# A hybrid decoder step on one core: sums of squares and two S5 table products moved from GpSimd to VectorE

## Chip, cores and metric

The kernel runs on 1 core of one Trainium2 chip. The metric is the device time of one execution in microseconds (us), taken as the median of several runs. A run is an execution of the whole program: one decoder layer for a prompt of 1024 tokens and a sample batch of 8 x 4 tokens, 1056 token columns in all.

The engines are TensorE (PE; its weight loads are PEld), VectorE (DVE), ScalarE (ACT), GpSimd (POOL) and SyncE (SP, which issues most DMAs). Each runs its own list of instructions in order and waits on semaphores for the others.

## The reference, cut to what matters here

One layer: an RMS norm, one input projection into attention, S5 and gate columns, attention and the S5 state-space branch, gates, output projection, MLP, final norm.

```python
def rmsnorm(x, g):
    xf = x.astype(jnp.float32)
    y = xf * lax.rsqrt(jnp.mean(xf * xf, axis=-1, keepdims=True) + RMS_EPS)
    return (y * g.astype(jnp.float32)).astype(x.dtype)
...
def s5_discretize(lam_re, lam_im, log_dt, b_re, b_im):
    """ZOH: A_bar = exp(dt*Lambda), B_bar = (A_bar - 1)/Lambda * B."""
...
    bb_re = f_re * b_re - f_im * b_im
    bb_im = f_re * b_im + f_im * b_re
    return ab_re, ab_im, bb_re, bb_im
...
    h = rmsnorm(x, g_mix)
    proj = h @ w_in
    q, k, v, u, gate_logits = jnp.split(
        proj, [D_ATTN, D_ATTN + D_KV, D_ATTN + 2 * D_KV, D_ATTN + 2 * D_KV + D_SSM], axis=-1)
```

The change touches the sum of the squares of x (for the norm), the product with `f_im` in `bb_re` and `bb_im`, and the product with the imaginary part of a power of `A_bar` that carries the sample states over four steps.

## The kernel before

Activations lie transposed: a tile has 128 of the 1024 channels as partitions and the 1056 tokens as columns, so x is eight tiles (k = 0 to 7). A product is made from three matmuls per k and chunk of 352 columns: high part of the weight by high part of the activation (L117), high by low (L118), low by high (L119). So each tile of x has a high part `hh` (ScalarE, L181, times the norm's weight) and a low part `hl` (VectorE, L182), and each weight block of 128x1024 a high part (ScalarE, L91) and a low part (VectorE, L92).

The part of the program that the change touches is its beginning:

- `start` (L166) loads x, makes `hh` and `hl`, squares each tile on ScalarE (L186) into one of three buffers `sq` and adds the squares up in `acc` (L188), on GpSimd.
- `first_tiles` (L500) multiplies two gate tiles with k outermost: for each k 18 matmuls of 128x352, 144 in all, into six banks of PSUM. So k waits for `hl[k]`.
- `token_norms` (L191) sums `acc` over the partitions on TensorE (L198), takes the root (L157 on ScalarE, the rest on VectorE) and spreads the result `r` over the partitions with TensorE (L207) into `rb`.
- `s5_params` (L266) is a long list of small VectorE instructions (64 or 32 columns) that discretise the state-space model; nine doublings of an angle (L374 to L381) are its end.
- `tile_in` (L506) makes one further tile of the projection: three banks of 24 matmuls each. Behind the first gate tiles come a gate tile and then the u tiles, whose banks VectorE moves out (`u_evac`, L435), times `rb`. Three banks (`mm`) go round, so the fourth u bank waits for nothing older than the first u bank, and the first bank of the third u tile for the evacuation of the fourth.
- `s5_tables` (L385) makes the table BB and the carried states FS, each from two products and a sum; one of the two products ran on GpSimd (L391, L402).
- `s5_a` (L537) and `s5_b` (L572) make per group of eight the matrices W2, V1, W1 and Kp, with a product on GpSimd beside VectorE each (L556, L568). Their memory (`s5work`) is that of the temporaries of `s5_params`, so the first `s5_a` waits for the last doubling. `s5_phases` (L404) makes tables of phases on VectorE (L420 to L425).

A scheduler sets the order of each engine's list when the program is built, from priorities and its own idea of how long things take; so an edit of an engine moves other instructions too. The numbers behind the names (mm_953, acc_174) tell tiles apart.

Of the kernel before, what the change touches and what calls it, by code (L numbers as in the profile page):

```python
# [12 lines left out]
ALU = mybir.AluOpType  # L13
# [32 lines left out]
def hybrid_kernel(tc, xt, cache_k, cache_v, h0, norms, w_in, sinks, w_attn_o, lam_re, lam_im, log_dt,  # L46
                  b_ri, b_ir, c_ri, d_cols, w_glu, w_out, w_up, w_down, w_last,
                  y_cols, y_rows, k_prompt, v_prompt, ssm_prompt, k_sample, v_sample, ssm_sample, dbg=None):
    nc = tc.nc
    uid = [0]  # L50

    def new(pool, shape, dt, tag, bufs=None):
        uid[0] += 1
        return pool.tile(list(shape), dt, tag=tag, name=f"{tag}_{uid[0]}", bufs=bufs)
# [47 lines left out]
    def prefetch(pool=wts):  # L102

        if len(loaded) < len(cols_in):
            kind, m = cols_in[len(loaded)]
            loaded.append(wblock(w_in, CB[kind] + m, pool=pool))
# [59 lines left out]
    def start(st, small_loads):  # L166

        nc.scalar.dma_start(gcol, norms)
        acc = new(st, [P, T], F32, "acc")
        xs = []  # L170
        for k in range(KT):
            x = new(st, [P, T], F32, "x", 8)
            nc.sync.dma_start(x, xt[k])
            if k in (0, PF2):
                prefetch(wts if k else st)
            if k == PF3:
                prefetch()
            if k == SLK:
                small_loads()
            g = gcol[:, 0, k:k + 1]  # L180
            nc.scalar.activation(hh[k], x, AF.Copy, scale=g)  # L181
            nc.vector.scalar_tensor_tensor(hl[k], x, g, hh[k].bitcast(F32), op0=ALU.mult, op1=ALU.subtract)  # L182
            xs.append(x)
        for k, x in enumerate(xs):
            sq = new(st, [P, T], F32, "sq", 3) if k else acc
            nc.scalar.activation(sq, x, AF.Square)  # L186
            if k:
                (nc.vector if k in AV else nc.gpsimd).tensor_tensor(acc, acc, sq, op=ALU.add)  # L188
        return acc

    def token_norms(st, acc):  # L191
# [17 lines left out]
            nc.scalar.copy(rb[:, 3 * c * P:3 * c * P + w], ps[:, :w])  # L209

    PF3 = 5
    AV, PF2, SLK = (), 1, 1


    AR0, AI0, R8 = 0, 9, 18
# [15 lines left out]
    def swap(dst, src, s0=1.0, s1=1.0):  # L231

        for d, s, sg in ((dst[0:64], src[64:128], s0), (dst[64:128], src[0:64], s1)):
            if sg == 1.0:
                nc.scalar.copy(d, s)
            else:
                nc.scalar.activation(d, s, AF.Copy, scale=sg)

    def s5_small_loads(pt):
        lr, li, ldt = (new(pt, [P, G], F32, t) for t in ("lr", "li", "dt"))  # L240
        nc.sync.dma_start(ldt, bass.AP(tensor=log_dt.tensor, offset=log_dt.offset, ap=[[0, P], [1, G]]))
        nc.sync.dma_start(lr, lam_re)
        nc.sync.dma_start(li, lam_im)
        return lr, li, ldt

    def s5_loads(pt):
        Y = new(slabA, [P, G, CH], F32, "slab")
        Ys = new(slabA, [P, G, CH], F32, "slab")
        dcol = new(pt, [P, KT, 2], F32, "dcol")
        q = S5Q  # L250
        q.dma_start(dcol, d_cols)
        q.dma_start(Y, b_ri)
        q.dma_start(Ys, b_ir)
        q.dma_start(XC, c_ri)
        q.dma_start(H0, h0)
        nc.gpsimd.memset(Up, 0.0)
        nc.gpsimd.memset(BBp, 0.0)
        nc.gpsimd.memset(Kp, 0.0)
        m16 = new(pt, [P, CH], F32, "m16")
        for i in range(4):  # L260
            nc.gpsimd.tensor_copy(m16[32 * i:32 * i + 32], ident[32 * i:32 * i + 32, 32 * i:32 * i + CH])
        nc.gpsimd.tensor_tensor(DD, m16[:, None, None, :].to_broadcast([P, KT, 2, CH]),
                                dcol[:, :, :, None].to_broadcast([P, KT, 2, CH]), op=ALU.mult)
        return Y, Ys
# [120 lines left out]
    def s5_tables(Y, Ys, fr, fi):  # L385
        nc.scalar.activation(XC[64:128], XC[64:128], AF.Copy, scale=-1.0)
        nc.scalar.activation(Ys[0:64], Ys[0:64], AF.Copy, scale=-1.0)

        sh = [P, G, CH]
        nc.vector.tensor_tensor(BB, Y, fr[:, :, None].to_broadcast(sh), op=ALU.mult)  # L390
        nc.gpsimd.tensor_tensor(Ys, Ys, fi[:, :, None].to_broadcast(sh), op=ALU.mult)  # L391
        nc.vector.tensor_tensor(BB, BB, Ys, op=ALU.add)

        H0s = new(slabA, [P, 4, SB, 16], F32, "slab")
        swap(H0s, H0, s0=-1.0)
        sh = [P, 4, SB, 16]

        def pw(col):
            return TP[:, col].rearrange("p (q g) -> p q g", q=4)[:, :, None, :].to_broadcast(sh)

        nc.vector.tensor_tensor(FS, H0, pw(AR0 + 4), op=ALU.mult)
        nc.gpsimd.tensor_tensor(H0s, H0s, pw(AI0 + 4), op=ALU.mult)  # L402
        nc.vector.tensor_tensor(FS, FS, H0s, op=ALU.add)
    def s5_phases(TE):  # L404

# [117 lines left out]
    with tc.tile_pool(name="ptmp", bufs=1) as pt:  # L523
        with tc.tile_pool(name="start", bufs=1) as st:
            prm = []
            acc = start(st, lambda: prm.extend(s5_small_loads(pt)))
            first_tiles()
            Y, Ys = s5_loads(pt)
            token_norms(st, acc)
            ft = s5_params(pt, *prm)  # L530
        for _ in range(NT0 - 2):
            tile_in()
        s5_tables(Y, Ys, *ft[:2])
# [589 lines left out]
    acc = new(const, [P, T], F32, "rb")  # L1123
# [94 lines left out]
    class Unit:  # L1218
# [5 lines left out]
        def prod(self, ps, i, start):  # L1224
            n = self.g.n
            w = self.g.w[i]
            for j in range(n):
                js = slice(j * P, j * P + P)
                b = self.right(j, i)
                for k, (wp, bp) in enumerate(((0, 0), (0, 1), (1, 0))):  # L1230
                    nc.tensor.matmul(ps[:, :CQ], w[:, wp, js], b[:, bp], start=start and j == k == 0,  # L1231
                                     stop=j == n - 1 and k == 2, skip_group_check=True)
# [396 lines left out]
```

## Time and profile before

| What | Value |
| --- | --- |
| median of 3 runs | 1742.67 us (1742.42 to 1746.3) |
| the profiled execution | 1745.46 us, span 1743.5 us |
| TensorE busy | 1664.1 us (95%) |
| VectorE busy | 1255.8 us (72%) |
| ScalarE busy | 863.0 us (49%) |
| GpSimd busy | 287.6 us (16%) |
| mean granted clock of TensorE | 0.978 |

The span goes from the first to the last instruction of the profiled execution; the 2 us around it belong to the execution too. A busy share is an average over stages. The change lies in the first 100 us, so the rows below are read from there: who waits for whom, what stands in which order on VectorE and GpSimd, and at which time TensorE starts a bank. Times are from the start of the span.

### The profile page before, as it was taken

To read this page: it belongs to the slowest core of one execution; us is meant where nothing else is said; L and a number is where in the kernel's file an instruction comes from. 1 tells how busy PE (TensorE), PEld (TensorE's weight loads), DVE (VectorE), ACT (ScalarE), POOL (GpSimd) and SP (SyncE) were. 2 spreads that over 40 slices of the span, in tenths; PEclk is the share of its full clock that TensorE was granted. 3 is DMA by queue.
4 is the path that set the end of the run, shared out by engine and by line. 5 is a ranking of instruction groups with operands and counts; after the bars stand their busy time and mean duration, and the time that the engine had idled before them with its cause. 6 is when DMAs were issued, how large, how long until landed. Compare 5 with 4: busy or idle time off the path is not lost. (4 is left out here: it accounts for less than half of the span.)

```text
span 1743.5 us, 30870 instructions
## 1 busy us (share of the span) xinstructions
PE 1664.1 (95%) x11952; PEld 1626.7 (93%) x11952; DVE 1255.8 (72%) x2449; ACT 863.0 (49%) x1878; POOL 287.6 (16%) x250
## 2 busy tenths in 40 slices
PE   6989999999999899999999999999999899999996
PEld 6989999999998888989999999999999899999986
DVE  8898787654488999842644767767776788777767
ACT  5344354332367788753433654444444555454454
POOL 5211111101234344420222320000000000000013
PEclk8999999999999999999999999999999999999998
DMA  5144434433101311133444544444444755453412
GB/s 205 62 149 149 127 94 142 141 110 108 51 25 54 109 50 62 62 123 98 143 132 132 178 144 137 155 148 136 136 148 137 248 159 155 126 165 113 124 55 100
DMA packets 131686, 213.16 MB, mean 122 GB/s; under 512 B 13756, under 2 KB 86540, under 8 KB 131028
## 3 DMA queue, kind: packets, MB, share of 16 engines
q1 hardware_dynamic: 84452, 162.16, 29.4%
q10 hardware_dynamic: 45360, 46.63, 7.9%
q0 software_dynamic: 1728, 2.41, 0.6%
q8 instruction: 93, 1.52, 0.4%
q14 instruction: 53, 0.43, 0.1%
HBM read 146.26 MB, written 64.90 MB: 121 GB/s over the span
## 5 line engine op out<-in xcount | busy, mean ns | idle before, releaser
L118 PE MATMUL mm<-slab,whi 128*128 128x352 f32 (+3 forms) x1688 | 532.0, 315 | 20.6 <-DVE slab L182 12.4
L117 PE MATMUL mm<-slab,whi 128*128 128x352 f32 (+3 forms) x1688 | 537.1, 320 | 8.2 <-DVE Up L435 7.1
L119 PE MATMUL mm<-slab,wlo 128*128 128x352 f32 (+3 forms) x1688 | 531.7, 315 | 0.3 <-DVE wlo L92 0.3
L1231 PE MATMUL ax<-slab,w 128*128 128x264 f32 x2880 | 371.4, 287 | 7.6 <-ACT slab L1394 4.9
L1231 PEld LDWEIGHTS ax<-slab,w 128*128 128x128 f32 x2880 | 360.7, 190 | 10.8 <-ACT slab L1394 5.3
L118 PEld LDWEIGHTS mm<-slab,whi 128*128 128x128 f32 x1688 | 322.4, 191 | 24.3 <-DVE slab L182 13.4
L117 PEld LDWEIGHTS mm<-slab,whi 128*128 128x128 f32 x1688 | 320.8, 190 | 10.9 <-issue 8.2
L119 PEld LDWEIGHTS mm<-slab,wlo 128*128 128x128 f32 x1688 | 321.2, 190 | 0.8 <-DVE wlo L92 0.6
L1231 PE MATMUL mm<-slab,w 128*128 128x264 f32 x2160 | 281.8, 286 | 9.2 <-DVE acc L1306 5.7
L1231 PEld LDWEIGHTS mm<-slab,w 128*128 128x128 f32 x2160 | 271.6, 190 | 11.9 <-DVE acc L1306 7.7
L91 ACT CAST whi<-raw 128x1024 fp32r<-128x1024 f32 x76 | 79.6, 1048 | 101.2 <-PE mm L118 64.9
L1526 POOL TENSOR_TENSOR slab<-slab,slab 128x512 f32<-128x512 f32 x7 | 9.1, 1293 | 659.2 <-ACT slab L1523 659.2
L1342 DVE TENSOR_TENSOR w<-raw,w 128x512 fp32r<-128x512 f32 (+2 forms) x96 | 63.0, 656 | 71.1 <-ACT w L1341 68.9
L92 DVE TENSOR_TENSOR wlo<-raw,whi 128x1024 fp32r<-128x1024 f32 x76 | 99.5, 1309 | 18.9 <-ACT whi L91 18.5
L1394 ACT CAST slab<-gt 128x528 fp32r<-128x528 f32 x98 | 62.0, 634 | 93.1 <-DMA gt<-ffd 91.3
L1395 DVE TENSOR_TENSOR slab<-gt,slab 128x528 fp32r<-128x528 f32 x98 | 68.5, 704 | 38.6 <-ACT slab L1394 38.2
L804 POOL TENSOR_TENSOR qs<-q,qs 64x256 fp32r<-64x256 f32 x64 | 62.9, 983 | 70.6 <-ACT qs L803 59.7
L1341 ACT CAST w<-whi 128x512 fp32r<-128x512 f32 (+2 forms) x64 | 37.9, 593 | 58.6 <-PE ax L1231 28.2
L828 ACT ACTIVATE pm<-pm,sm 128x128 f32<-128x128 f32 x128 | 49.9, 391 | 33.6 <-DVE sm L825 33.4
L1255 ACT ACTIVATE slab<-slab 128x264 f32<-128x264 f32 x80 | 33.9, 425 | 61.8 <-DVE slab L1254 45.4
L843 POOL TENSOR_TENSOR pt<-fb,pt 128x512 fp32r<-128x512 f32 x28 | 41.6, 1485 | 120.2 <-ACT pt L842 76.7
L1341 ACT CAST w<-raw 128x512 fp32r<-128x512 f32 (+2 forms) x96 | 56.9, 593 | 4.8 <-PE mm L1231 2.5
(400 smaller groups left out, 2649.8 us busy)
## 6 DMA issues: line engine op xcount, KB each, us to landing
gt<-ffd SPq DMA_DIRECT2D x106, 264.0 KB
raw<-in_w_in_dram SPq DMA_DIRECT2D x36, 512.0 KB
raw<-in_w_up_dram SPq DMA_DIRECT2D x32, 512.0 KB
ffd<-slab ACTq DMA_DIRECT2D x28, 528.0 KB
raw<-in_w_down_dram SPq DMA_DIRECT2D x22, 512.0 KB
gd<-gt ACTq DMA_DIRECT2D x48, 176.0 KB
slab<-gd SPq DMA_DIRECT2D x16, 528.0 KB
raw<-in_w_glu_dram SPq DMA_DIRECT2D x16, 512.0 KB
```

Source lines behind the costliest of these rows:

```text
L91: nc.scalar.copy(hi[:, :nk], raw[:, :nk])
L92: nc.vector.tensor_tensor(lo[:, :nk], raw[:, :nk], hi[:, :nk].bitcast(F32), op=ALU.subtract)
L117: nc.tensor.matmul(ps[:, :cw], w[0][:, k, :], ah[k][:, cs], start=(k == 0), stop=False)
L118: nc.tensor.matmul(ps[:, :cw], w[0][:, k, :], al[k][:, cs], start=False, stop=False)
L119: nc.tensor.matmul(ps[:, :cw], w[1][:, k, :], ah[k][:, cs], start=False, stop=(k == nk - 1))
L804: nc.gpsimd.tensor_tensor(qs[b, :, h], q[a, :, bs], qs[a, :, h].bitcast(F32), op=ALU.subtract)
L828: nc.scalar.activation(pm[:, i], pm[:, i], AF.Exp, bias=ng[:, i:i + 1], accum_out=den[:, i:i + 1])
L1231: nc.tensor.matmul(ps[:, :CQ], w[:, wp, js], b[:, bp], start=start and j == k == 0, stop=j == n - 1 and k == 2, skip_group_check=True)
L1341: nc.scalar.copy(t[:, 0], s)
L1342: V.tensor_tensor(t[:, 1], s, t[:, 0].bitcast(F32), op=ALU.subtract)
L1394: nc.scalar.copy(f[:, 0], ft)
L1395: V.tensor_tensor(f[:, 1], ft, f[:, 0].bitcast(F32), op=ALU.subtract)
```

## The change

Three edits: the adds of the squares (L188), the product L391 of BB and the product L402 of FS are issued on VectorE. The set `AV`, which could send some of the adds to VectorE and was empty, goes.

```diff
             if k:
-                (nc.vector if k in AV else nc.gpsimd).tensor_tensor(acc, acc, sq, op=ALU.add)
+                nc.vector.tensor_tensor(acc, acc, sq, op=ALU.add)
...
-    AV, PF2, SLK = (), 1, 1
+    PF2, SLK = 1, 1
...
-        nc.gpsimd.tensor_tensor(Ys, Ys, fi[:, :, None].to_broadcast(sh), op=ALU.mult)
+        nc.vector.tensor_tensor(Ys, Ys, fi[:, :, None].to_broadcast(sh), op=ALU.mult)
...
-        nc.gpsimd.tensor_tensor(H0s, H0s, pw(AI0 + 4), op=ALU.mult)
+        nc.vector.tensor_tensor(H0s, H0s, pw(AI0 + 4), op=ALU.mult)
```

VectorE's list at the start, from the low part of the second weight block on, before (slab_106 and slab_107 are the low parts of k = 2 and 3; ek, er, ep and den belong to `s5_params`):

```order
L92 TENSOR_TENSOR wlo_190<-raw_187,whi_189 128x1024
L278 TENSOR_SCALAR ek_129_482<-ek_129_482 128x64
L345 TENSOR_TENSOR den_585<-den_585,ta_529 128x64
L279 SCALAR_TENSOR_TENSOR er_130_483<-ek_129_482,ex_132_485 128x64
L281 TENSOR_SCALAR ei_133_486<-ek_129_482 128x64
L346 RECIPROCAL den_585<-den_585 128x64
L280 SCALAR_TENSOR_TENSOR er_130_483<-ek_129_482,er_130_483 128x64
L282 TENSOR_SCALAR ep_131_484<-er_130_483 128x64
L284 SCALAR_TENSOR_TENSOR ep_131_484<-ep_131_484,er_130_483 128x64
L182 SCALAR_TENSOR_TENSOR slab_106<-x_201,gcol_79,slab_98 128x1056
L284 SCALAR_TENSOR_TENSOR ep_131_484<-ep_131_484,er_130_483 128x64 x4
L182 SCALAR_TENSOR_TENSOR slab_107<-x_205,gcol_79,slab_99 128x1056
```

The same place of VectorE's list now:

```order
L92 TENSOR_TENSOR wlo_190<-raw_187,whi_189 128x1024
L188 TENSOR_TENSOR acc_174<-acc_174,sq_232 128x1056
L278 TENSOR_SCALAR ek_129_482<-ek_129_482 128x64
L345 TENSOR_TENSOR den_585<-den_585,ta_529 128x64
L279 SCALAR_TENSOR_TENSOR er_130_483<-ek_129_482,ex_132_485 128x64
L182 SCALAR_TENSOR_TENSOR slab_106<-x_201,gcol_79,slab_98 128x1056
L188 TENSOR_TENSOR acc_174<-acc_174,sq_235 128x1056
L182 SCALAR_TENSOR_TENSOR slab_107<-x_205,gcol_79,slab_99 128x1056
L188 TENSOR_TENSOR acc_174<-acc_174,sq_238 128x1056
L182 SCALAR_TENSOR_TENSOR slab_108<-x_209,gcol_79,slab_100 128x1056
L188 TENSOR_TENSOR acc_174<-acc_174,sq_241 128x1056
```

Adds and low parts alternate up to the last of each, and the small instructions from L280 on stand behind all of them.

VectorE's list around the evacuation of the fourth u bank (mm_953) and the fifth (mm_979), before, from the last sum of the first `s5_a` group on:

```order
L569 TENSOR_TENSOR tmp_897<-tmp_897,tmp_898 128x1024
L424 TENSOR_TENSOR slab_902<-slab_902,slab_904 128x8x32
L425 TENSOR_TENSOR slab_903<-slab_903,slab_904 128x8x32
L420 TENSOR_TENSOR slab_902<-slab_902,slab_604 128x8x4
...
L424 TENSOR_TENSOR slab_902<-slab_902,slab_904 128x8x16
L425 TENSOR_TENSOR slab_903<-slab_903,slab_904 128x8x16
L435 TENSOR_TENSOR Up_122<-mm_953,rb_80 128x44x8
L435 TENSOR_TENSOR Up_122<-mm_979,rb_80 128x44x8
```

The same two evacuations on VectorE now, from the sum L557 of W2 on:

```order
L557 TENSOR_TENSOR W_182_885<-W_182_885,tmp_893 128x1152
L422 TENSOR_TENSOR slab_903<-slab_903,slab_604 128x8x4
L423 TENSOR_TENSOR slab_904<-slab_902,slab_604 128x8x4
L424 TENSOR_TENSOR slab_902<-slab_902,slab_904 128x8x4
L435 TENSOR_TENSOR Up_122<-mm_953,rb_80 128x44x8
L425 TENSOR_TENSOR slab_903<-slab_903,slab_904 128x8x4
...
L569 TENSOR_TENSOR tmp_897<-tmp_897,tmp_898 128x1024
L422 TENSOR_TENSOR slab_903<-slab_903,slab_604 128x8x8
...
L425 TENSOR_TENSOR slab_903<-slab_903,slab_904 128x8x16
L435 TENSOR_TENSOR Up_122<-mm_979,rb_80 128x44x8
```

The evacuation of mm_953 moved ahead of L569 and of ten phase operations, and these now stand between it and the evacuation of mm_979.

TensorE's list at the end of the second u tile (mm_1005) and in the first bank of the third (mm_1094), as a difference; L579 and L585 are the transposes and small products of `s5_b`:

```order
 L119 MATMUL mm_1005<-slab_103,wlo_778 128x352
-L579 MATMUL ax_1041<-ident_72,tmp_897 128x128 x4
-L579 MATMUL ax_1047<-ident_72,tmp_897 128x128 x4
-L585 MATMUL ax_1053<-W_182_885,BBp_123 32x128 x8
 L117 MATMUL mm_1094<-slab_96,whi_864 128x352
 L118 MATMUL mm_1094<-slab_104,whi_864 128x352
...
 L117 MATMUL mm_1094<-slab_99,whi_864 128x352
+L579 MATMUL ax_1041<-ident_72,tmp_897 128x128 x4
+L579 MATMUL ax_1047<-ident_72,tmp_897 128x128 x4
+L585 MATMUL ax_1053<-W_182_885,BBp_123 32x128 x8
 L118 MATMUL mm_1094<-slab_107,whi_864 128x352
```

The transposes moved from ahead of that bank to behind its tenth matmul.

## Rows read from the trace of the kernel before

**Rows 1.** The page's part on busy time: busy us, share, instructions.

```profile
PE 1664.1 (95%) x11952; PEld 1626.7 (93%) x11952; DVE 1255.8 (72%) x2449; ACT 863.0 (49%) x1878; POOL 287.6 (16%) x250
```

**Rows 2.** Waits of PE, whole span: total us, times, longest us.

```profile
PE mm L118 <- DVE slab L182: 12.4, 2, 10.5
PE mm L117 <- DVE Up L435: 7.1, 1, 7.1
PE ax L680 <- DVE FP L670: 5.1, 3, 3.4
```

**Rows 3.** Stretches: length, busy us of PE to POOL, clock, DMA share, GB/s.

```profile
16.00:18.00 2.00, 0.00 (x0) 0.00 (x0) 2.00 (x4) 2.00 (x3) 1.92 (x2) 0.88 1.03 406
...
28.00:30.00 2.00, 2.00 (x8) 2.00 (x8) 1.97 (x2) 0.00 (x0) 1.92 (x2) 0.50 0.00 0
```

**Rows 4.** Timeline of the start: start us, us, instruction, idle before.

```profile
12.20 10.17 POOL L188 TENSOR_TENSOR acc<-acc,sq 128x1056 f32<-128x1056 f32 x4 [7.88 <-ACT sq L186]
...
12.44 2.47 DVE L278 TENSOR_SCALAR ek<-ek 128x64 f32<-128x64 f32 x1
...
22.60 3.48 DVE L182 SCALAR_TENSOR_TENSOR slab<-x,gcol,slab 128x1056 fp32r<-128x1056 f32 x1
...
26.52 4.95 POOL L188 TENSOR_TENSOR acc<-acc,sq 128x1056 f32<-128x1056 f32 x2
```

**Rows 5.** Timeline of DVE with GpSimd idle.

```profile
36.04 1.31 DVE L182 SCALAR_TENSOR_TENSOR slab<-x,gcol,slab 128x1056 fp32r<-128x1056 f32 x1
37.27 1.22 DVE L92 TENSOR_TENSOR wlo<-raw,whi 128x1024 fp32r<-128x1024 f32 x1
```

**Rows 6.** Line L1083: ns min/median/max, first and last start.

```profile
L1083 DVE TENSOR_TENSOR slab<-q,slab x8: 1241/1244/2736, 832.6 to 843.6; 128x1056 fp32r<-128x1056 f32 x8
```

**Rows 7.** Timeline of PE at the waits and bank starts named.

```profile
26.13 0.66 PE L118 MATMUL mm<-slab,whi 128*128 128x352 f32 x1 [10.53 <-DVE slab L182]
...
28.36 0.49 PE L118 MATMUL ax<-slab,whi 128*128 128x352 f32 x1
28.65 0.49 PE L119 MATMUL ax<-slab,wlo 128*128 128x352 f32 x1
...
33.09 0.43 PE L118 MATMUL mm<-slab,whi 128*128 128x352 f32 x1 [1.90 <-DVE slab L182]
...
49.06 1.99 PE L198 MATMUL ax<-ones,acc 128*128 128x1 f32 x18
...
98.47 0.63 PE L117 MATMUL mm<-slab,whi 128*128 128x352 f32 x1 [7.06 <-DVE Up L435]
...
104.39 0.32 PE L117 MATMUL mm<-slab,whi 128*128 128x352 f32 x1
104.55 0.33 PE L118 MATMUL mm<-slab,whi 128*128 128x352 f32 x1
...
125.53 0.41 PE L117 MATMUL mm<-slab,whi 128*128 128x352 f32 x1
```

**Rows 8.** Timeline of DVE beside GpSimd's products L391 and L402.

```profile
55.07 1.93 DVE L365 COPY es<-su 64x32 f32<-64x32 f32 x1
...
64.73 1.30 DVE L375 TENSOR_TENSOR hb<-slab 128x32 f32<-128x32 f32 x1
```

**Rows 9.** Timeline of DVE and POOL around the first s5_a.

```profile
76.12 0.17 DVE L381 TENSOR_TENSOR slab<-ha,hr 128x32 f32<-128x32 f32 x1
...
77.14 5.14 POOL L556 TENSOR_TENSOR tmp<-xc,TP 128x1152 f32<-128x1152 f32 x1 [11.16 <-DVE Up L435]
...
78.14 1.99 DVE L567 TENSOR_TENSOR tmp<-BB,TP 128x1024 f32<-128x1024 f32 x1
...
88.94 2.48 DVE L425 TENSOR_TENSOR slab<-slab,slab 128x256 f32<-128x256 f32 x1
...
91.34 2.51 DVE L420 TENSOR_TENSOR slab<-slab,slab 128x32 f32<-128x32 f32 x1
```

**Rows 10.** Waits of DVE from 98 to 200 us: total, times, longest.

```profile
DVE ep L620 <- DMA ab<-abd: 3.0, 2, 2.0
```

## Prediction

> **What bounds the kernel now.** TensorE is busy for 95% of the span [rows 1], so an edit on VectorE and GpSimd counts only where TensorE waits for them. The list of TensorE's waits comes first [rows 2]: 12.4 us for the low parts hl (L182), 7.1 us for the evacuation of the u tiles (L435), both in the first 100 us, and then small ones. The first is one wait of 10.53 us that ends at 26.13 and one of 1.90 us that ends at 33.09 [rows 7].
>
> Why are the low parts late? In the timeline of those microseconds the reader is to see VectorE and GpSimd side by side [rows 4]. While GpSimd adds squares, from 12.20 to 31.47 with little between, a VectorE instruction of 64 columns takes 2.47 us and a low part 3.48 us. With GpSimd idle the low part takes 1.31 us and the next instruction starts 1.23 us after it [rows 5]. So VectorE gets one or two instructions in for each add of 2.46 us. The table of stretches rules out the transfers as the cause [rows 3]: at 16 to 18 us the DMA share is full, at 28 to 30 us it is zero, and VectorE is held in both. It also shows the clock: granted 0.88 falling to 0.50 (1.2 GHz of 2.4) after TensorE stops.
>
> **Part 1, the seven adds.** Their price on VectorE has a row: an elementwise operation of 128x1056 with two inputs takes 1.24 us (median of eight) [rows 6], so 1.16 us from start to start, 8.1 us for seven. What they give back is the hold. From 12.44 to the end of the last add, 31.47, lie 19.0 us, in which VectorE's own work is one low part and some 14 small ones (0.13 to 0.2 us each free of holds, the reciprocal 0.5), about 3.5 us: 15.5 us of hold go.
>
> TensorE gets this. In the new order add and low part alternate, so low parts come 1.23 + 1.16 = 2.4 us apart, with one weight split of 1.13 us among them. The first add stands at 12.44, three small ones follow, and the third low part starts at 14.0 and ends at 15.3, when TensorE still has work (it ran dry at 15.60) [rows 7]. The others end at 17.7, 20.1, 23.6, 26.0 and 28.4, the last add at 29.7. TensorE needs 18 matmuls of 0.16 us, 2.9 us, for each, so it is the slower of the two. Of its 144 matmuls 105 are left at 15.60: 105 x 0.161 = 16.9 us, end at 32.5, so the column sums of L198 start at 32.7 where they started at 49.06 [rows 7]. **That is 16.4 us earlier**: 12.4 us of waits and 4.0 us of matmuls at 0.29 in place of 0.16 us.
>
> **Part 2, the two products.** On VectorE they cost 1.14 us (1024 columns, by [rows 6]) and 0.6 us (half of it). The holds that they end are 1.75 us of the 1.93 and 1.1 us of the 1.30 that a copy and a product of 32 columns took [rows 8], since such take 0.18. Net -1.1 us. With the adds VectorE's own account is 18.4 us of hold less 9.8 us of work, **8.6 us**.
>
> **Part 3, what VectorE now owes.** TensorE is 16.4 us early, VectorE only 8.6 us, so it is asked how far the lead survives; this is the term where I chose.
> L198 ends at 34.6 (before 51.05). From there to the last small product of the ninth doubling (L381), which frees the memory of s5_a, VectorE took 25.2 us (76.30) [rows 9]. Now: 25.2, less the two holds 2.85, plus the two products 1.74, plus some 65 small discretisation instructions that before ran ahead of 49 us among the last low parts (9.2 us at 0.13 to 0.15), plus two evacuations and a weight split that the new order puts ahead (2.6), plus waits for TensorE's banks (1.3): 37.2, so 71.9.
> Then L555 and L567 (to 75.2), GpSimd's product of s5_a, which waits for L567 and ends 2.15 us behind it, as at 82.28 behind 80.13 [rows 9] (77.4), L557 and three small ones: the evacuation of the fourth u bank starts at 79.0 and ends at 79.8. TensorE has finished its six banks at 73.2 (34.6, then nine banks of 3.87, L207 2.3 and 1.5 for a slow clock after L198) and waits 6.6 us, as long as before: it goes on at 79.85 where it was 98.47, 18.6 early.
> Three things take from this. The transposes of s5_b (1.6 us, before ahead of the wait) now stand behind ten matmuls of the next bank. The idle time brings the low clock, as after 98.47, where 24 matmuls took until 104.39. And the evacuation of the fifth bank now stands behind L569 and ten small operations, and GpSimd's next three products hold these, 2.5 us each as in [rows 9]: L569 81.9 to 83.1, two holds to 88.4, seven small ones, evacuation 89.9 to 90.7. TensorE is ready for that bank at 79.85 + 2.9 (ten at 0.29) + 0.3 + 2.4 + 2.3 = 87.8 and waits to 90.8, 13.6 early against 104.39. If this idle of 3 us costs 11 matmuls at the low clock, as the wait to 33.09 did, 1.4 us go: **12.2 us** at the bank that started at 125.53. VectorE evacuates the bank that this one needs at 112.8, TensorE wants it at 113.3.
> Behind that VectorE has idle time of its own in the trace of before (3.0 us for the copy of the phase table alone, 98 to 200 us) [rows 10], and GpSimd's and ScalarE's work there is the same, in the same order; nothing later is tied to a fixed time, since loads go by freed buffers. So I let 12 us pass to the end.
>
> The Trainium skill, page VectorE: DVE Perf Modes, section The DRAIN you can't avoid, says that a VectorE operation does not start until the pipe of the one ahead is empty. By it each of the nine would cost its whole duration, 0.08 us more, 0.7 us in all, and the time would be 1731.4. The trace disagrees: L92 starts at 37.27, L182 ahead of it ends at 37.35 [rows 5]; so the pitch stands.
>
> **The rivals.**
> *The whole first gain stays.* If the small operations slip in between GpSimd's products, the fifth bank is evacuated in time and only the transposes count: its 16.2 us remain, 1742.7 - 16.2 = 1726.5. Against it: two of them, at 88.94 and 91.34, were held 2.5 us each [rows 9].
> *VectorE sets the pace through all of S5.* Then its own account is all that counts, 8.6 us: 1734.1. For it: in both stretches of [rows 3] VectorE is full, and it stays so but for the waits named to 100 us. Against: the idle time behind that [rows 10].
> *A later wait takes it.* The waits of TensorE for FP in the S5 stage (5.1 us in all) [rows 2] could grow by most of what was won: some 2 us remain, 1740.7. Against: by my walk HB of the first group comes 13.8 us earlier, more than the 12.2 of TensorE.
> *Slower.* If the long VectorE instructions come of something other than GpSimd (the loads that fill the first 25 us), nothing is given back, and seven adds of 1.16 us stand ahead of the low parts for which TensorE waits at 15.6: 8.1 us later, 1750.8. It decides if a low part still takes over 2.5 us at 15 us. Against: VectorE is held at 28 to 30 us too, without any DMA [rows 3], and with DMA gone and GpSimd idle a low part takes 1.31 us [rows 5].
> The Trainium skill, page SBUF — State Buffer, section SBUF: two separate sides, says that DMA and engines do not meet at the memory and that only VectorE and GpSimd share a port pair, which one of them locks for a whole instruction. By this rule the slower case falls away; the trace agrees in the two stretches named.
> That the adds stay on GpSimd is no rival: the order shows nine rows gone from its list.
>
> **How the numbers follow.** The profiled execution took 1745.5 us with a span of 1743.5; less 12 its span would be 1731.5. The median of the runs is 1742.67, so I forecast 1742.67 - 12 = 1730.7. Chances: forecast 0.56 (1728 to 1733), whole gain 0.14, VectorE's account 0.18, a later wait 0.08, slower 0.04. A measurement of this kernel tells 0.3%, 5.2 us, from no change. Faster by more: 0.56 + 0.14 + 0.17 = 0.87; within: 0.09; slower: 0.04. The range goes from the far end of the whole gain (1725) to between VectorE's account and the later wait (1738).
>
> **What would show it.** Right: the wait for L182 gone from TensorE's list, L198 near 32.5, L182 at 1.3 us throughout; a wait for L435 of 6 to 7 us that ends near 80 and a second of about 3 us near 91; the start of the bank behind L649 near 113. Wrong: if TensorE runs dry again before 30 us (part 1), if L381 ends away from 72 (part 3), if the second wait is missing or over 5 us, or if the lead shrinks between 120 us and the end.

## The result, and the profile after

The changed kernel takes 1730.55 us (median of 4 runs, 1729.53 to 1731.69) against 1743.62 us of the kernel before in the same runs: a ratio of 0.9915 with a 95% interval of 0.9894 to 0.9936. That is 13.1 us faster, where 12 us were forecast. The profiled execution took 1729.53 us, its span 1727.8 us.

The page's part on busy time (busy us, share, instructions), against [rows 1]: GpSimd has lost 22.7 us of busy time and nine instructions, VectorE has nine more and is busy for 9.6 us less, since a hold (the time that a VectorE operation takes beyond what it takes with GpSimd idle) counts as busy.

```profile
PE 1659.0 (96%) x11952; PEld 1620.5 (94%) x11952; DVE 1246.2 (72%) x2458; ACT 864.5 (50%) x1878; POOL 264.9 (15%) x241
```

TensorE's list of waits (total us, times, longest), against [rows 2]: the wait for L182 is gone from it, the wait for L435 is two waits now, and the one for FP is 0.8 us longer.

```profile
PE mm L117 <- DVE Up L435: 8.2, 2, 5.9
...
PE ax L680 <- DVE FP L670: 5.9, 3, 3.4
```

The two stretches of [rows 3] in the changed kernel (length, busy us of PE, PEld, DVE, ACT and POOL, clock, DMA share, GB/s). The DMA share from 16 to 18 us is the same as before (1.03), but GpSimd's column is empty, TensorE is full, and its granted clock is 1.00 where it was 0.88 and 0.50.

```profile
16.00:18.00 2.00, 2.00 (x14) 2.00 (x13) 2.00 (x3) 2.00 (x3) 0.00 (x0) 1.00 1.03 406
28.00:30.00 2.00, 2.00 (x15) 2.00 (x14) 2.00 (x2) 0.00 (x0) 0.00 (x0) 1.00 0.07 27
```

VectorE's timeline of those microseconds (start, us, instruction), against [rows 4]: L278 takes 0.19 us where it took 2.47, a low part 1.31 where it took 3.48, and the adds lie between them. One low part alone is longer, 1.68 us: it starts while GpSimd's only operation of that time, L262, still runs (the POOL row). With the last of these rows, at 30.06, the small instructions start.

```profile
12.62 1.25 DVE L188 TENSOR_TENSOR acc<-acc,sq 128x1056 f32<-128x1056 f32 x1
13.79 0.19 DVE L278 TENSOR_SCALAR ek<-ek 128x64 f32<-128x64 f32 x1
...
14.16 1.31 DVE L182 SCALAR_TENSOR_TENSOR slab<-x,gcol,slab 128x1056 fp32r<-128x1056 f32 x1
15.39 1.25 DVE L188 TENSOR_TENSOR acc<-acc,sq 128x1056 f32<-128x1056 f32 x1
...
21.53 1.53 POOL L262 TENSOR_TENSOR DD<-m,dcol 128x256 f32<-128x256 f32 x1 [17.21 <-DMA dcol<-in_d_cols_dram]
22.49 1.68 DVE L182 SCALAR_TENSOR_TENSOR slab<-x,gcol,slab 128x1056 fp32r<-128x1056 f32 x1
...
30.06 0.22 DVE L280 SCALAR_TENSOR_TENSOR er<-ek,er 128x64 f32<-128x64 f32 x1
```

TensorE's timeline at the places of [rows 7] (idle time before the row in brackets). L198 starts 16.35 us earlier, the third u tile (78.06) 20.4 us, and the bank behind the first L649 (111.69, before 125.53) 13.84 us. Between the last two lies the second wait, 2.34 us.

```profile
32.71 1.99 PE L198 MATMUL ax<-ones,acc 128*128 128x1 f32 x18
...
78.06 0.63 PE L117 MATMUL mm<-slab,whi 128*128 128x352 f32 x1 [5.89 <-DVE Up L435]
...
96.72 0.40 PE L117 MATMUL mm<-slab,whi 128*128 128x352 f32 x1 [2.34 <-DVE Up L435]
...
109.92 2.01 PE L649 MATMUL ax<-U,W 128*128 128x136 f32 x16
111.69 0.41 PE L117 MATMUL mm<-slab,whi 128*128 128x352 f32 x1
```

VectorE and GpSimd around the first two s5_a, against [rows 9]: the reader is to see which VectorE rows are long. L567 is held by the product that started at 71.16 (3.98 us; the next L567, at 88.72 with GpSimd idle, takes 1.99), L425 once by the next product and once by the third; the evacuation L435 at 77.14 takes 0.78 us though GpSimd has just begun its product. At 94.69 it is no hold: VectorE waits for the result of GpSimd's fourth product, which started only at 92.12, and the evacuation that TensorE needs stands behind that sum.

```profile
70.12 0.20 DVE L381 TENSOR_TENSOR slab<-ha,hr 128x32 f32<-128x32 f32 x1
...
71.16 2.74 POOL L556 TENSOR_TENSOR tmp<-xc,TP 128x1152 f32<-128x1152 f32 x1 [48.10 <-ACT xc L237]
71.69 3.98 DVE L567 TENSOR_TENSOR tmp<-BB,TP 128x1024 f32<-128x1024 f32 x1
...
77.08 2.55 POOL L568 TENSOR_TENSOR tmp<-bbs,TP 128x1024 f32<-128x1024 f32 x1 [3.19 <-DVE W L557]
77.14 0.78 DVE L435 TENSOR_TENSOR Up<-mm,rb 128x352 f32<-128x352 f32 x1
77.72 1.96 DVE L425 TENSOR_TENSOR slab<-slab,slab 128x32 f32<-128x32 f32 x1
...
79.88 1.21 DVE L569 TENSOR_TENSOR tmp<-tmp,tmp 128x1024 f32<-128x1024 f32 x1
...
81.23 2.37 POOL L556 TENSOR_TENSOR tmp<-xc,TP 128x1152 f32<-128x1152 f32 x1 [1.60 <-DVE tmp L569]
81.42 2.27 DVE L425 TENSOR_TENSOR slab<-slab,slab 128x64 f32<-128x64 f32 x1
...
84.82 1.39 DVE L435 TENSOR_TENSOR Up<-mm,rb 128x352 f32<-128x352 f32 x2
...
88.72 1.99 DVE L567 TENSOR_TENSOR tmp<-BB,TP 128x1024 f32<-128x1024 f32 x1
90.62 1.35 DVE L557 TENSOR_TENSOR W<-W,tmp 128x1152 f32<-128x1152 f32 x1
...
92.12 2.54 POOL L568 TENSOR_TENSOR tmp<-bbs,TP 128x1024 f32<-128x1024 f32 x1 [8.51 <-DVE HB L666]
94.69 1.23 DVE L569 TENSOR_TENSOR tmp<-tmp,tmp 128x1024 f32<-128x1024 f32 x1 [2.69 <-POOL tmp L568]
```

Behind each of the two waits the clock is low, as the table of stretches shows (columns as above, the clock is 0.56 and 0.66).

```profile
79.00:85.00 6.00, 6.00 (x37) 4.99 (x37) 6.00 (x15) 2.85 (x8) 3.00 (x2) 0.56 0.01 3
...
97.00:102.00 5.00, 5.00 (x23) 5.00 (x22) 5.00 (x6) 1.72 (x4) 1.33 (x1) 0.66 0.30 73
```

### The profile page after: what moved, and what is told of

The parts are those of the page before. It is cut to its first block, busy times and chain, and to the rows that moved or that the text cites. A ratio compares the mean times of both kernels' runs of the same rounds, so it can differ in the third digit from the quotient of the medians.

```text
span 1727.8 us, 30869 instructions
## 1 busy us (share of the span) xinstructions
PE 1659.0 (96%) x11952; PEld 1620.5 (94%) x11952; DVE 1246.2 (72%) x2458; ACT 864.5 (50%) x1878; POOL 264.9 (15%) x241
## 5 line engine op out<-in xcount | busy, mean ns | idle before, releaser
L118 PEld LDWEIGHTS mm<-slab,whi 128*128 128x128 f32 x1688 | 321.1, 190 | 11.8 <-DVE slab L986 9.0
```

Of the source, the lines that this page charges most:

```text
L118: nc.tensor.matmul(ps[:, :cw], w[0][:, k, :], al[k][:, cs], start=False, stop=False)
```

## The experiments

All twelve ran apart from the result above, in groups, each group beside its own runs of the kernel before, whose times there lie up to 0.6% from their median. So each run is given by its ratio to the kernel before and by its **lead**: by how much earlier VectorE's instructions start than the same ones in the trace before, as the median over those that start between 500 and 550 us in that trace (93 of them). By then the S5 stage, which ends at about 400 us, is over. The changed kernel's lead is 14.9 us in the profile above and 13.3 us in the control below; the mean granted clock up to 420 us is 0.98 in the one and 0.97 in the other. So a difference of 1.6 us between two leads, each of one execution, says nothing by itself.

### Which part carries the gain

The adds alone, with the two products left on GpSimd:

```diff
-        nc.vector.tensor_tensor(Ys, Ys, fi[:, :, None].to_broadcast(sh), op=ALU.mult)
+        nc.gpsimd.tensor_tensor(Ys, Ys, fi[:, :, None].to_broadcast(sh), op=ALU.mult)
-        nc.vector.tensor_tensor(H0s, H0s, pw(AI0 + 4), op=ALU.mult)
+        nc.gpsimd.tensor_tensor(H0s, H0s, pw(AI0 + 4), op=ALU.mult)
```

> Only the seven adds on VectorE; the products L391 and L402 stay on GpSimd. Theory (the adds carry the gain; the products are worth about 1.1 us of VectorE's account, which sets the end of the wait for L435): the wait for L182 is gone, L198 starts at 32.7 us, the ninth L381 about 1 us later than the 70.1 of the changed kernel, the wait for L435 of 5.9 us about 1 us longer, 1731 to 1732.5 us. Rival (the gain needs both parts, since VectorE's lead at the ninth L381 counts alone): 1735 us or more.

Measured: 1728.91 against 1746.42 us, ratio 0.9898 (0.9869 to 0.9926), lead 11.5 us. L198 starts at 32.66, the ninth L381 at 71.72, 1.6 us later than in the changed kernel, and both waits for L435 are longer, as TensorE's timeline shows:

```profile
79.70 0.63 PE L117 MATMUL mm<-slab,whi 128*128 128x352 f32 x1 [7.59 <-DVE Up L435]
...
98.48 0.63 PE L117 MATMUL mm<-slab,whi 128*128 128x352 f32 x1 [3.05 <-DVE Up L435]
```

The products alone, with the adds on GpSimd:

```diff
-                nc.vector.tensor_tensor(acc, acc, sq, op=ALU.add)
+                nc.gpsimd.tensor_tensor(acc, acc, sq, op=ALU.add)
```

> Only the two products L391 and L402 on VectorE; the seven adds stay on GpSimd. Theory: the wait for L182 stays at 12.4 us, the wait for L435 shrinks from 7.1 to about 6 us, since VectorE is 1.1 us ahead there: 1741 to 1743 us against 1743.6. Rival (the products carry a good part of the gain): 1737 us or less. Rival (they only cost VectorE time): 1744.5 us or more.

Measured: 1744.85 against 1746.42 us, ratio 0.9990 (0.9970 to 1.0010), lead 0.2 us. TensorE's waits:

```profile
PE mm L118 <- DVE slab L182: 13.1, 2, 10.5
...
PE mm L117 <- DVE Up L435: 5.4, 1, 5.4
```

The adds carry the gain. The products shorten the wait for L435 by 1.7 us (7.1 to 5.4), as they do beside the adds (7.6 to 5.9), but alone none of it is left at 500 us. Beside the adds some 2 us are likely, by the leads (11.5 us against 13.3 and 14.9) and by the waits for L435 (10.6 us in all against 8.5 and 8.2); the ratios don't show them.

### Is it GpSimd's work that holds VectorE?

The changed kernel, in which GpSimd adds the squares as well, for nothing:

```diff
                 nc.vector.tensor_tensor(acc, acc, sq, op=ALU.add)
+                nc.gpsimd.tensor_tensor(Up.rearrange('p t n -> p (t n)')[:, 0:T], sq, sq, op=ALU.add)
```

> The changed kernel, and GpSimd adds each square to itself as well, seven operations of 128x1056 into memory that is cleared later, whose result nobody reads. Theory (GpSimd's operations hold VectorE, whoever needs them): the low part is again 2.5 to 3.7 us long while GpSimd adds, TensorE waits for L182 some 12 to 20 us again, and VectorE has its own 8 us of adds on top: 1743 to 1752 us. Rival (the long VectorE operations came of the loads, or of the order of the list, and GpSimd's work beside it costs nothing): 1730 to 1732 us.

Measured: 1744.71 against 1746.42 us, ratio 1.0004 (0.9983 to 1.0024), lead -1.1 us. VectorE's timeline, with the same list as the changed kernel, and TensorE's list of waits (lines below 188 are one further down here):

```profile
12.28 3.00 DVE L188 TENSOR_TENSOR acc<-acc,sq 128x1056 f32<-128x1056 f32 x1
15.20 1.93 DVE L279 TENSOR_SCALAR ek<-ek 128x64 f32<-128x64 f32 x1
...
25.66 3.00 DVE L182 SCALAR_TENSOR_TENSOR slab<-x,gcol,slab 128x1056 fp32r<-128x1056 f32 x1
```

```profile
PE mm L117 <- DVE Up L436: 10.0, 4, 6.1
PE mm L118 <- DVE slab L182: 9.9, 3, 4.9
```

Seven operations that nobody needs take the whole gain away; neither the loads nor the order of VectorE's list are different here, and VectorE waits for nobody from 9 to 43 us, so its operations are long and not late. The total fell where it was expected, but the wait for L182 is 9.9 us and not 12 to 20: five adds and low parts take 3.00 us, some 1.7 over their own time, and two small operations 1.9 to 2.0, in all 12 us of hold, less than the 15.5 of the kernel before. With the adds on VectorE as well it comes late to the evacuations too, and the wait for these (L436 here) grows from 8.2 to 10.0 us.

### What the adds still cost

```diff
             if k:
-                nc.vector.tensor_tensor(acc, acc, sq, op=ALU.add)
```

> The seven adds are left out, on every engine (the sum of squares is then that of the first tile alone, so the norm is another); the two products stay on VectorE. It measures what the adds still cost where they are. Theory (up to L198 TensorE is the slower engine, behind it VectorE): L198 starts at 32.5 us as in the changed kernel, the small instructions start 8 us earlier, the ninth L381 comes near 62 to 64 us, the wait of 5.9 us for L435 goes, with 1 to 2 us of low clock: 1722 to 1726 us. Rival (the adds lie beside TensorE's work for nothing): 1730 us.

Measured: 1727.14 against 1746.42 us, ratio 0.9899 (0.9869 to 0.9928), lead 18.0 us. L198 starts at 32.49, as with the adds: up to there they cost TensorE nothing. The ninth L381 comes at 61.40, 8.7 us earlier than in the changed kernel, as expected. But the wait for L435 does not go. VectorE's timeline (L421 to L423 are the phase operations L423 to L425, L433 is the evacuation L435) and TensorE's:

```profile
69.51 2.56 DVE L423 TENSOR_TENSOR slab<-slab,slab 128x32 f32<-128x32 f32 x1
...
73.53 2.28 DVE L421 TENSOR_TENSOR slab<-slab,slab 128x64 f32<-128x64 f32 x1
75.74 2.56 DVE L422 TENSOR_TENSOR slab<-slab,slab 128x64 f32<-128x64 f32 x1
...
79.57 1.34 DVE L433 TENSOR_TENSOR Up<-mm,rb 128x352 f32<-128x352 f32 x2
```

```profile
80.45 0.63 PE L117 MATMUL mm<-slab,whi 128*128 128x352 f32 x1 [5.39 <-DVE Up L433]
```

The scheduler has put this evacuation behind the phase operations, three of which GpSimd's products hold for 2.3 to 2.6 us each. So 8.7 us of VectorE are worth 3 to 5 us of lead (18.0 against 14.9 and 13.3); the ratio can't tell them from none.

### The next place: s5_a

The waits for L435 that are left stand behind s5_a, so the next runs put its products on VectorE, and the second u tile ahead of it, beside a control. The control is the changed kernel once more:

> The changed kernel once more, as the control for the three runs beside it. Any theory: as before, 0.9915 of the time of the kernel before, with the waits for L435 of 5.9 and 2.3 us in the first 100 us.

Measured: 1731.40 against 1745.19 us, ratio 0.9920 (0.9896 to 0.9943), lead 13.3 us, waits for L435 of 8.5 us in all, the longest 5.4.

The second u tile first:

```diff
+    tile_in()
     w2 = s5_a(0)
     s5_phases(ft[2])
-    tile_in()
```

> The changed kernel with the second u tile written ahead of the first s5_a and the phase table, so that two of its three bank evacuations stand ahead of L555 and L567 on VectorE. Theory (the wait of 5.9 us for L435 comes of the place of one evacuation behind s5_a on VectorE): it goes, with 1 to 2 us of low clock, and of this 2 to 4 us come back where the first bank of the u tile after next waits behind L569 and the phase operations: 3 to 6 us faster than the changed kernel. Rival (the wait is VectorE's total work up to s5_b, so it only moves): within 1.5 us of the changed kernel.

Measured: 1734.61 us, ratio 0.9933 (0.9908 to 0.9958), lead 11.5 us. TensorE's list of waits:

```profile
PE ax L579 <- DVE tmp L569: 7.4, 1, 7.4
...
PE mm L117 <- DVE Up L435: 3.7, 2, 2.8
```

The wait of 5.9 us went, and one of 7.4 us for the last sum of the same s5_a came in its place. The theory fell. The rival's mechanism is what the waits show, that the place of the evacuation only decides where VectorE's lateness appears; its 1.5 us can't be checked at this scatter (3.2 us slower than the control, within the intervals).

s5_a's products on VectorE, in all eight groups:

```diff
-        gp, V = nc.gpsimd, nc.vector
+        gp, V = nc.vector, nc.vector
```

> The changed kernel with both products of each s5_a (L556, L568) on VectorE too. Theory (a product of GpSimd costs VectorE some 2 us of hold and 1.2 us of its own work if it is moved, but the scheduler now puts the evacuation of the fourth u bank behind L568, L569 and twelve phase operations): the first wait for L435 grows from 5.9 to 8 to 10 us, the second of 2.3 us goes, the total within 3 us of the changed kernel. Rival (to take any work from GpSimd that VectorE's operations meet gives time): 4 us or more faster than the changed kernel.

Measured: 1721.34 us, ratio 0.9866 (0.9843 to 0.9888), lead 23.3 us. The theory fell, the rival holds: 10 us more than the control. In the first group TensorE's wait is 6.95 us, before L579, no shorter than the 5.9 of the changed kernel; the gain lies behind it. Both edits together:

> The two edits together: s5_a's products on VectorE and the second u tile written ahead. Theory: neither wait for L435 is left over 3 us, so it is the fastest, 5 to 9 us faster than the changed kernel. Rival (VectorE's account sets the pace, and 2.3 us more of work for each group costs more than the holds of about 4 us that go): the tile order alone is as fast or faster.

Measured: 1720.02 us, ratio 0.9855 (0.9831 to 0.9879), lead 23.2 us: the tile order adds nothing that can be told, though the wait before L579 is 2.5 us. The two edits are 11 us faster than the control, more than the theory's 5 to 9, and the rival fell.

Which groups? The edit for the first group alone, and for the other seven alone:

```diff
-        gp, V = nc.gpsimd, nc.vector
+        gp, V = (nc.gpsimd if m else nc.vector), nc.vector
```

> The changed kernel with s5_a's two products on VectorE for the first group of eight alone. Theory (the first 100 us of S5 hold only part of what the move of all products gave, 10 us): the one or two waits there are 7 us in all as with all products moved, and the gain over the changed kernel is 2 to 4 us. Rival (all of the gain is in the first group): 8 us or more.

```diff
-        gp, V = nc.gpsimd, nc.vector
+        gp, V = (nc.vector if m else nc.gpsimd), nc.vector
```

> The changed kernel with s5_a's two products on VectorE for the later seven groups, and on GpSimd for the first. Theory: the wait of 5.9 us for the fourth u bank stays, the one of 2.3 us behind the second group's L569 goes, and so does part of the waits for FP (L670, 5.9 us): 5 to 8 us faster than the changed kernel. Rival: within 2 us of it.

Measured: the first group 1730.35 us, ratio 0.9921 (0.9894 to 0.9949), lead 12.7 us: nothing, so theory and rival both fell. The later groups **1716.26 against 1745.55 us, ratio 0.9844 (0.9814 to 0.9874)**, lead 25.5 us: the lowest median of all, 12 us of lead beyond the control where 5 to 8 us were expected. TensorE's list of waits for the later groups:

```profile
PE mm L117 <- DVE Up L435: 6.1, 2, 6.0
...
PE ax L680 <- DVE FP L670: 2.6, 3, 1.3
```

The wait of 5.9 us stays, the second one is gone, and that for FP is halved. These are some 6 us less of waits than in the changed kernel; the mean granted clock up to 420 us is 0.99 where the control has 0.97, by an estimate 0.02 x 420 = 8 us of full clock, a part of which falls into waits, so it is large enough for the other 6 us. VectorE has 15.8 us more of busy time from 100 to 420 us for it (246.2 against 230.4), and no longer waits for GpSimd, as it did six times there, 16.4 us in all.

Is it that wait? Only the second product of the later groups on VectorE:

```diff
-        gp.tensor_tensor(tv, ov1(bbs), pv1(AI0), op=ALU.mult)
+        (V if m else gp).tensor_tensor(tv, ov1(bbs), pv1(AI0), op=ALU.mult)
```

> The changed kernel with only the second product of s5_a (L568, for V1) on VectorE in the later seven groups; the first (L556) stays on GpSimd. In the changed kernel VectorE waits for L568 in front of L569 six times from 100 to 420 us, 16.4 us in all, and never for L556. Theory (most of the gain of moving both, some 12 us at 500 us, comes of that wait, not of the holds by L556): 9 to 12 us faster than the changed kernel. Rival (the holds by L556, about 2 us in each group, weigh as much as the wait): 4 to 7 us faster.

Measured: 1728.33 against 1745.43 us, ratio 0.9904 (0.9874 to 0.9934), lead 13.7 us, 0.4 us more than the control. Theory and rival both fell. VectorE's wait for L568 is gone, but TensorE waits again for evacuations, as its list up to 420 us shows:

```profile
PE mm L117 <- DVE Up L435: 11.6, 5, 5.9
PE ax L680 <- DVE FP L670: 3.2, 3, 2.0
PE ax L680 <- DVE HB L669: 2.5, 1, 2.5
```

The list was ordered anew in each of these kernels, so it stays open whether the product that is left takes the gain by its hold or the new order does.

Do the two gains add? The kernel before, with s5_a's products on VectorE in all groups:

> The kernel before, adds and table products on GpSimd, with s5_a's products of all groups on VectorE. Theory (holds in different stages are paid one by one where TensorE waits for VectorE, so the gains add): about 8 to 10 us faster than the kernel before, and the wait for L182 stays at 12.4 us. Rival (VectorE is late by the same total, and what is not freed at the start is still owed in S5): 4 us or less.

Measured: 1733.63 against 1745.55 us, ratio 0.9937 (0.9915 to 0.9958), lead 12.1 us, the wait for L182 12.9 us. The theory's 8 to 10 us are 12.1, and the rival fell. 12.1 and the control's 13.3 make 25.4; both edits together have 23.3. So they add, as nearly as leads can tell: what GpSimd's work costs in a stage is paid in that stage.

## Why the prediction was right, and where it was not

**The hold and what it gives back (part 1)** was right in its mechanism and its size. The echo run shows that GpSimd's operations alone make VectorE's long. L198 was forecast for 32.7 and came at 32.71, 16.35 us earlier than before (forecast 16.4). The third low part was to end at 15.3 and ended at 15.47, the last add was to end at 29.7 and ended at 30.1. Low parts were to take 1.3 us throughout, and all but the one beside L262 did. TensorE did not run dry, and its clock stayed at the high level.

**The products (part 2)** were to be worth 1.1 us of VectorE's account. The ninth L381 is 1.6 us later without them. Beside the adds they are worth some 2 us of lead, little more than two leads of one kernel differ by; alone, 0.2 us.

**What VectorE still owes (part 3)** was the term where a choice was made, and it held: TensorE again waits for the fourth u bank, 5.89 us (forecast 6.6), until 78.06 (79.85). The step that was off is the walk to the end of the ninth L381: 37.2 us forecast, 35.6 taken (34.70 to 70.32). Its 1.3 us of waits for TensorE's banks did not come; VectorE's list of waits has none there behind the one for L198 itself. TensorE came to the wait 1.0 us early too (72.17, forecast 73.2): the sum has 1.5 us of low clock behind L198, and the granted clock from 34 to 40 us is 1.00. In the first s5_a the hold lay the other way round than walked: L567 waited for GpSimd's product and not the product for L567. L557 starts 5.2 us behind the ninth L381 (5.5 walked), so this cost nothing, by luck.

**The second wait** came, but not where it was put. Forecast was a wait of 3 us that ends at 90.8, for the fifth u bank, with two of the ten phase operations behind L569 held, by the third and the fourth of GpSimd's products. The third did hold one (81.42). The fourth had followed the third at once in the kernel before:

```profile
91.10 2.71 POOL L568 TENSOR_TENSOR tmp<-bbs,TP 128x1024 f32<-128x1024 f32 x1
```

In the changed kernel it started only at 92.12, after 8.51 us in which GpSimd waited for VectorE, whose L557 of that group ends at 91.97 and L666 right behind it; which buffer it waited for is not shown. So the second hold was missing, and the evacuation at 84.82 came 5 us earlier than walked. TensorE found that bank free. It stopped two banks later instead, for 2.34 us, because the same product was late: L569 of the second s5_a waited 2.69 us for its result, with the evacuation behind it. TensorE had some 11 matmuls at 0.29 in place of 0.16 us there: the price, 3.8 us, is near the 4.4 us of the forecast (3 of wait, 1.4 of clock) by another mechanism. That is luck of the sum: the fourth product was charged as a hold and cost as a wait. With all of this the bank behind L649 was 1.6 us early (111.69, forecast 113.3).

**The rest of the program** passed the lead on: 13.84 us at the bank behind L649, 14.9 us at 500 us, 13.1 us in the medians. Of the rivals, the whole first gain (16.2 us) did not stay, VectorE's own account (8.6 us) was too little, no wait behind 120 us in the S5 stage grew by more than 0.8 us (FP), and the slower case, that loads make VectorE's operations long, falls with the first two stretches shown above: a DMA share of 1.03 and low parts of 1.31 us. The Trainium skill, page VectorE: DVE Perf Modes, section The DRAIN you can't avoid, adds to the sentence that the prediction sets against the trace that operations which it calls not held start earlier; so the 0.08 us between 37.27 and 37.35 do not speak against that section.

What the prediction did not see is what GpSimd's products in s5_a cost. It read them as given and looked only for the waits that they cause near 90 us; to move them gave 10 to 12 us of lead, about as much as the adds had. Whether they cost it by their holds, by VectorE's waits for their results or by the order of the lists stays open.

## What to carry to other kernels

When VectorE's small operations take the time of a GpSimd operation, price the GpSimd work by what it holds and not by what it computes: here an add cost VectorE some 2.2 us while GpSimd made it (15.5 us of hold for seven) and 1.16 us when VectorE made it itself. A gain on the engine that is waited for passes on until that engine is late again, so walk its list to the next wait, and then to the one behind it. And walk GpSimd's list beside it, with GpSimd's own waits: a hold counts only where GpSimd's operation really stands. Here one product came 8.5 us later than the row it was read from suggests, and a forecast hold became a wait for its result.

## What was not expected of the hardware

**The evacuations, which read PSUM, are not held.** In the rows above the evacuation at 77.14 takes 0.78 us while GpSimd's product runs from 77.08 to 79.63 (0.79 us at 57.21, with GpSimd idle), and the next operation of two SBUF inputs, which starts before that product ends, takes 1.96 us for 32 columns. The Trainium skill, page SBUF — State Buffer, section SBUF: two separate sides, says that a VectorE operation contends with GpSimd where it has two SBUF inputs and GpSimd's operation reads SBUF, or where its mode takes both port pairs; the trace agrees.

**A lead changes by several us with no difference in code.** Behind 600 us the lists of the kernel before and of the one with the adds alone are the same, yet the lead of the latter goes from 11.8 us (950 to 1000 us) to 14.6 us (1100 to 1150). The table of stretches shows the granted clock for it, first in the kernel before, then with the adds alone, whose work there is 12 us earlier. Each of the two stretches holds the same idle time of 2.8 us and all of the low clock around it (the clock is 1.00 in the 30 us behind each): 0.83 against 0.94 in 30 us, 3.3 us. With s5_a's later groups moved, the lead grows from 25.5 us to 31.9 at 950, on lists that are the same behind 420 us; from 550 to 950 us its clock is 1.00, that of the kernel before 0.98.

```profile
1030.00:1060.00 30.00, 27.23 (x187) 26.62 (x186) 18.60 (x48) 14.94 (x33) 2.19 (x3) 0.83 0.13 44
```

```profile
1000.00:1030.00 30.00, 27.23 (x215) 26.82 (x214) 19.52 (x41) 15.85 (x30) 8.06 (x7) 0.94 0.43 144
```

So for an edit of the first stages the lead at their end tells more than the median of the runs, where it changes by more than the 1.6 us by which the leads of one kernel differed here.
